# A planned order of TensorE work: later due times for FFN transposes and first scores, and a last update in two pieces

## Chip, cores and metric

The kernel runs on one core of a Trainium2 chip. The metric is the device time of one execution in microseconds. All weights (some 220 MB) stream from HBM once per execution.

## The reference

Two blocks on x of 256 tokens by 1024, in float32. The first has two layers, each:

```
x = x + 0.5 * swiglu(rms_norm(x, ffn1_norm), w_gate, w_up, w_down)
h = rms_norm(x, mix_norm)
pa, pb, pc, pd = split(h @ w_in)
ya, yb, yc, yd = neighbourhood(pa), latent(pb), differential(pc), grouped(pd)
x = x + concat(ya, yb, yc, yd) @ w_out
x = x + 0.5 * swiglu(rms_norm(x, ffn2_norm), ...)
x = rms_norm(x, final_norm)
```

swiglu is (silu(h @ w_gate) * (h @ w_up)) @ w_down with an inner width of 2816. The four mixers are attentions of four heads each over all 256 tokens, with different norms, biases and rotations. The second block is one layer of three gated branches (pooling, windowed attention with sinks, causal attention), `x + merged @ w_out`, and a last rms_norm, which gives the output.

## The kernel before, in words

**Products.** Every large product is made in three matmuls of fp32r: weights and activations are split into a high part and a rest (hi, lo and xTh, xTl), and hi·hi, hi·lo and lo·hi are added up in PSUM (`acc`, L339). A matmul takes 128 rows of the inner dimension, one token tile t (128 tokens; there are two) and up to 512 output columns. Weights come in units of 128 x 1024 (512 KB): a transfer on SyncE's queue into one of three staging buffers `st`, then a "cut": ScalarE writes hi, VectorE writes lo (`Weights.cut`, L194). Six pairs hi/lo are alive at a time.

**The stages of a layer.** `ffn` (L546) goes over six chunks of 512 (the last 256) inner columns; for each it makes the gate product and the up product for both token tiles with `proj` (L496). `ev_gate` (L553) writes fg = silu(gate) on ScalarE; `ev_up` (L557) writes fh = up * rstd * fg on VectorE into one buffer per token tile, and spawns the transposes of fh: `trans_split` (L394) transposes four 128 x 128 tiles on TensorE into a PSUM tile tps, from which ScalarE writes hTh and VectorE hTl. When all chunks are done, `wide` (L521) makes the down product from hTh and hTl over 22 rows of tiles. `mixers` (L712) makes the input projections of the four head groups in the order differential, latent, neighbourhood, grouped, and spawns a generator for each; the output projection is again `wide` over eight row tiles in the order 4, 5 (differential), 2, 3 (latent), 0, 1 (neighbourhood), 6, 7 (grouped), each as soon as its rows yT are there (`before`, L1072). The next FFN starts with the gate product of token tile 0.

**A head group.** `softmax_pv` (L572) works through jobs (a pair of heads and a token tile): `scores` (two PSUM tiles sps, row maximum on VectorE, exponential E on ScalarE), `transposes` of E (evicted as PT), `values` (evicted as yt), `finish` (transposed back into y). When a token tile's jobs are done, `post` normalises y to yn and transposes it into yT. A group takes the turn at L673 (`att["busy"]`) and gives it back when the transposes of its last job are issued (L701). The second block has two such groups, `moba` (L1178) and `swa` (L1199).

**The order of the work.** The program is written out in one order by a planner. `Clock` (L61) estimates, for TensorE, ScalarE, VectorE and GpSimd, when each operation would end; `clock.pe` is its TensorE time and `clock.last` the estimated end of what an eviction or a step issued. A generator given to `spawn` (L410) has a due time: at the first opportunity after `clock.pe` has passed it, its next step is issued between the matmuls of the running product (`tick`, L446, called after each three or six matmuls). By default the due time is `clock.last`. Transfers count as arriving 1.4 us apart. `drain_until` (L453) runs background steps until a condition holds and moves the planner's TensorE time ahead if nothing is due. The framework then orders each engine's queue by program order and by what its own estimate has ready; operations that read PSUM are lifted by 14 places (L151 to L153).

**The end.** `last` (L1308) takes each finished piece of the last product (t, h), h the half of 512 columns: VectorE adds it to x, ScalarE squares it with a running sum, VectorE multiplies by the final gain into xg. After h = 1 the two sums are added, scaled and raised to -0.5 on GpSimd (`rpow`, L348), VectorE scales the first half and SyncE sends it, ScalarE scales the second and sends it from its own queue. In a row of the trace, L153 and L154 are the helper through which all VectorE, ScalarE and GpSimd operations go (with and without a PSUM operand), L333 is every matmul and L337 every transpose.

Of the kernel before, what the change touches and what calls it, by code (L numbers as in the profile page):

```python
# [10 lines left out]
F = mybir.dt.float32  # L11
R = mybir.dt.float32r
ACTF = mybir.ActivationFunctionType
ALU = mybir.AluOpType
# [3 lines left out]
D = 1024  # L18
DFF = 2816
L = 2  # L20
EPS = 1e-6
# [18 lines left out]
FIRST = [1, 1, 2, 2, 2]  # L40
WARM = 6
AHEAD = 14
OUT_ORDER = (4, 5, 2, 3, 0, 1, 6, 7)
IN2 = {"ax": 0, "az": 512, "bq": 1024, "bkv": 1536, "bz": 1792,
       "cq": 2304, "ck": 2816, "cv": 3328, "cz": 3840, "g": 4352}
# [79 lines left out]
class Engine:  # L125
# [5 lines left out]
    def __getattr__(self, op):  # L131
        f = getattr(self._eng, op)

        def call(*args, **kw):
# [16 lines left out]
            if not sb:  # L151
                with self._tc.high_priority(AHEAD):
                    return f(*args, **kw)  # L153
# [76 lines left out]
def decoder(ctx, tc, a, out):  # L230
    nc = tc.nc
    clock = Clock()
    act, dve, gps = (Engine(e, n, clock, tc) for e, n in (
        (nc.scalar, "act"), (nc.vector, "dve"), (nc.gpsimd, "pool")))
    PSUM = bass.MemoryType.PSUM

    def pool(name, bufs, stack=ctx, **kw):
        return stack.enter_context(tc.tile_pool(name=name, bufs=bufs, **kw))
# [13 lines left out]
    stat = pool("stat", 3)  # L252
# [6 lines left out]
    mhalf = const.tile([128, 16], F, name="mhalf")  # L259
# [4 lines left out]
    for l in range(L):  # L264
        for f in (1, 2):
            if f == 2:
# [8 lines left out]
                ws.add(wi, 8, 512, 2, (OFF_GQA, OFF_GQA + 512))  # L275
                for k in OUT_ORDER:
                    ws.add(a["w_out"][l][k * 128:(k + 1) * 128, :], 1, D, 1)
            for c in range(0, DFF, 512):
                n = min(512, DFF - c)
# [13 lines left out]
    x = keep.tile([128, 2, D], F, name="x")  # L293
# [11 lines left out]
    def tok(t):  # L305
        return slice(t * 128, (t + 1) * 128)

    def half(h):
        return slice(h * 512, (h + 1) * 512)
# [16 lines left out]
    def load_gain(ap):  # L326
        g = gain_p.tile([128, D], F, tag="g", name="gain")
        nc.sync.dma_start(out=g, in_=ap.partition_broadcast(128))
        return g
# [18 lines left out]
    def rpow(ss, n, inv, tag):  # L348

        m = stat.tile([128, n], F, tag=f"m{tag}{n}", name="ms")  # L350
        dve.tensor_scalar(m, ss, inv, EPS, op0=ALU.mult, op1=ALU.add)
        r = stat.tile([128, n], F, tag=f"r{tag}{n}", name="r")
        if n < 4:
            gps.tensor_tensor(out=r, in0=m, in1=mhalf[:, :n], op=ALU.pow)
            return r
        I = mybir.dt.int32
        dve.tensor_scalar(r.bitcast(I), m.bitcast(I), -0.5, float(0x5f3759df), op0=ALU.mult,
                          op1=ALU.add)
        q = stat.tile([128, 16], F, tag="q", name="q", bufs=1)[:, :n]
        for _ in range(3):  # L360
            dve.scalar_tensor_tensor(out=q, in0=m, scalar=-0.5, in1=r, op0=ALU.mult,
                                     op1=ALU.mult)
            dve.tensor_tensor(out=q, in0=q, in1=r, op=ALU.mult)
            dve.scalar_tensor_tensor(out=r, in0=q, scalar=1.5, in1=r, op0=ALU.add, op1=ALU.mult)
        return r

    def square_sum(src, tag):
        junk = junk_p.tile([128, D], mybir.dt.bfloat16, tag="junk", name="junk")
        ss = stat.tile([128, 1], F, tag="ss" + tag, name="ss")
        act.activation(out=junk[:, :src.shape[1]], in_=src, func=ACTF.Square, accum_out=ss)  # L370
        return ss
# [7 lines left out]
    def scaled(out, ps, s):  # L379
        act.activation(out=out, in_=ps, func=ACTF.Copy, scale=s)  # L380
# [29 lines left out]
    def spawn(gen, first=False, at=None):  # L410
        at = clock.last if at is None else at
        bg.insert(0 if first else len(bg), [gen, at, at])

    def timed(f, *args):

        before, clock.last = clock.last, 0.0
        f(*args)
        end = clock.last
        clock.last = max(before, end)
        return end  # L420
# [21 lines left out]
    def step(f, *args):  # L442
        f(*args)
        yield
# [101 lines left out]
    def ffn(norm_out, first=None):  # L546
        hTh = big.tile([128, KF, S], R, tag="bigA", name="hTh")
        hTl = big.tile([128, KF, S], R, tag="bigB", name="hTl")
        for c in range(6):
            n = min(512, DFF - 512 * c)  # L550
            g = {}

            def ev_gate(t, ps):  # L553
                g[t] = wk.tile([128, 512], F, tag=f"fg{t}", name="fg", bufs=1)
                act.activation(out=g[t][:, :n], in_=ps[:, :n], func=ACTF.Silu, scale=rstd[t])

            def ev_up(t, ps):  # L557
                h = wk.tile([128, 512], F, tag=f"fh{t}", name="fh", bufs=1)
                dve.scalar_tensor_tensor(out=h[:, :n], in0=ps[:, :n], scalar=rstd[t],
                                         in1=g[t][:, :n], op0=ALU.mult, op1=ALU.mult)  # L560
                ks = slice(4 * c, 4 * c + n // 128)
                spawn(step(trans_split, hTh[:, ks, tok(t)], hTl[:, ks, tok(t)], h[:, :n]), True)

            proj(8, n, first if first and c == 0 else 1024 // n, ev_gate, skew=c == 0)
            proj(8, n, 1024 // n, ev_up)
        wide(range(KF), hTh, hTl, [1] * (KF - 4) + [4],
             lambda t, h, ps: norm_out.update(t, h, ps, 0.5), lambda k, t: k < KF - 2 or not bg)
# [4 lines left out]
    def softmax_pv(jobs, post, scored=None, have_v=lambda: True):  # L572
# [3 lines left out]
        n = len(jobs)  # L576
# [95 lines left out]
        e_at, p_at, y_at = {}, {}, {}  # L672
        yield lambda: not att["busy"]  # L673
        att["busy"] = True
        while i4 < n:
            now = clock.pe
            nxt = [now + 300]
            if i4 < i3:
                nxt.append(y_at[i4])
            if i3 < i2:  # L680
                nxt.append(p_at[i3])
            if i2 < i1:
                nxt.append(e_at[i2])
            if i4 < i3 and y_at[i4] <= now:
                end = timed(finish, i4)
                t = jobs[i4]["t"]
                if post and (i4 == n - 1 or jobs[i4 + 1]["t"] != t):
                    spawn(post(t), True, end)
                i4 += 1
                yield 0  # L690
            elif i3 < i2 and p_at[i3] <= now and i3 == i4 and have_v():
                y_at[i3] = timed(values, i3)
                att["pt"] -= 1
                i3 += 1
                yield 0
            elif i2 < i1 and att["pt"] < 2 and e_at[i2] <= now:
                p_at[i2] = timed(transposes, i2)
                att["pt"] += 1
                i2 += 1
                if i2 == n:  # L700
                    att["busy"] = False  # L701
                yield 0
            elif i1 < n and i1 - i2 < 2 and (i1 == 0 or e_at[i1 - 1] <= now + 300):
                e_at[i1] = timed(scores, i1)
                i1 += 1
                if i1 == n and scored:
                    scored()
                yield 0
            else:
                yield max(now + 100, min(nxt))  # L710

    def mixers(l, cols, rows, nlam, norm_out):  # L712
# [108 lines left out]
        def latent(um, w):  # L821
# [96 lines left out]
            for t in range(2):  # L918
                for p in range(2):
# [4 lines left out]
                        v=[[v[:, k, h, 0:64] for k in range(2)] for h in hs],  # L924
                        y=heads(y[:, t, tok(p)])))
            yield from softmax_pv(jobs, post_rms(y, "mla_beta", 2), lambda: finished.add("mla_s"))

        def differential(u, v):
# [143 lines left out]
        def before(k, t):  # L1072
            k0 = k // 2 * 2
            return (k0, t) in finished and (k0 == 6 or (k0, 1) in finished)
        wide(OUT_ORDER, yTh, yTl, [1] * 4 + [4], lambda t, h, ps: norm_out.update(t, h, ps, 1.0),
             before)
# [20 lines left out]
    for l in range(L):  # L1097
        ffn(Norm(gains[:, 3 * l + 1]), FIRST if l == 0 else None)
        if l == 0:
            nc.sync.dma_start(out=cst, in_=a["cst"].rearrange("(t p) c -> p t c", p=128))  # L1100
            for n in (3, 6):
                dve.tensor_tensor(out=gains[:, n], in0=gains[:, n], in1=gains[:, 7 + n // 6],
                                  op=ALU.mult)
# [200 lines left out]
            fin2.add("c")  # L1304
    gf = load_gain(a["final_norm_g_2"])
    ss, xg = {}, {}

    def last(t, h, ps):  # L1308
        sl = x[:, t, half(h)]
        dve.tensor_tensor(out=sl, in0=ps, in1=sl, op=ALU.add)  # L1310
        ss[t, h] = square_sum(sl, f"x{h}")
        if h == 0:
            xg[t] = xg_p.tile([128, D], F, tag="xg", name="xg")
        dve.tensor_tensor(out=xg[t][:, half(h)], in0=sl, in1=gf[:, half(h)], op=ALU.mult)
        if h == 1:
            dve.tensor_tensor(out=ss[t, 0], in0=ss[t, 0], in1=ss[t, 1], op=ALU.add)
            r = rpow(ss[t, 0], 1, 1.0 / D, f"x{t}")
            dve.tensor_scalar(xg[t][:, half(0)], xg[t][:, half(0)], r, None, op0=ALU.mult)
            nc.sync.dma_start(out=out[tok(t), half(0)], in_=xg[t][:, half(0)])
            scaled(xg[t][:, half(1)], xg[t][:, half(1)], r)  # L1320
            nc.scalar.dma_start(out=out[tok(t), half(1)], in_=xg[t][:, half(1)])

    wide(range(8), mTh, mTl, [4, 4], last)


# [118 lines left out]
```

## Time and profile before

| what | value |
|---|---|
| median of 3 runs | 1319.79 us (1315.48 to 1320.84) |
| the profiled execution, its own time | 1318.63 us |
| its span, first to last instruction | 1316.5 us |
| TensorE busy | 1291.3 us, 98% |
| weight loads (beside the matmuls) | 1046.1 us, 79% |
| VectorE, ScalarE, GpSimd busy | 792.7, 722.5, 28.6 us |
[...]
| transfers | 221.80 MB, 168 GB/s |

The profiled execution spent 1318.63 - 1316.5 = 2.1 us outside its span. Busy time of a matmul overlaps with the next, so groups of matmuls are read by the time from start to start: 0.227 us for 512 columns at the full clock. A row of a timeline gives the start, the duration, the engine, and in brackets the idle time of the engine before it and what ended it.

### The profile page before, as it was taken

The page shows a single profiled execution, that of the slowest core. Times are in us where ns is not written, and L with a number is a line of the kernel's source. Part 1 is how long each engine was busy: PE and PEld are TensorE (multiplying, and loading weights), DVE is VectorE, ACT ScalarE, POOL GpSimd, SP SyncE. Part 2 cuts the span into 40 slices and gives each one's busy share as a digit, 9 for nine tenths or more (in the row PEclk, how much of TensorE's full clock was granted, in tenths as well). Part 3 has the DMA queues.
Part 4 walks back from the last instruction along what each step waited for, and adds up shares of the span by engine and source line. Part 5 has one row for each costly group of instructions (what it writes and reads, how often), then busy time and mean ns, then how long its engine had stood idle before and what let it go on. Part 6 is the DMA issues. An engine that isn't in the chain of part 4 may idle for free.

```text
span 1316.5 us, 17826 instructions
## 1 busy us (share of the span) xinstructions
PE 1291.3 (98%) x6514; PEld 1046.1 (79%) x6514; DVE 792.7 (60%) x1615; ACT 722.5 (55%) x1223; POOL 28.6 (2%) x44
## 2 busy tenths in 40 slices
PE   8999999999999999999999999999999999999997
PEld 7788888766788888788888876678888887678886
DVE  5655449895655544755545798565554565555475
ACT  6544437866644444644435676664444466566543
POOL 0000001000000000100000000000000000000000
PEclk9999999999999999999999998999999999999999
DMA  8766657432566665666665733156667474245652
GB/s 278 219 181 188 183 166 238 126 97 65 172 190 184 183 188 164 208 183 188 186 186 167 218 115 98 45 179 189 185 181 235 144 234 127 80 145 168 205 170 80
DMA packets 109815, 221.80 MB, mean 168 GB/s; under 512 B 7456, under 2 KB 30368, under 8 KB 109728
## 3 DMA queue, kind: packets, MB, share of 16 engines
q1 hardware_dynamic: 109152, 220.04, 55.5%
q8 instruction: 51, 0.84, 0.3%
q10 hardware_dynamic: 576, 0.63, 0.1%
q14 instruction: 36, 0.29, 0.1%
HBM read 219.59 MB, written 1.05 MB: 168 GB/s over the span
## 4 chain that ended last, share of the span: by engine, by line
PE 82%; DMA 6%; DVE 5%; ACT 4%; issue 1%; POOL 1%; SPq 0%; POOLq 0%; ACTq 0%; DVEq 0%
PE mmps L333 71%; PE tps L337 6%; PE sps L333 3%; DMA st<-in_w_in_dram 3%; PE tps L333 3%; DVE lo L154 2%; ACT hi L154 2%; DMA st<-in_ffn_w_gate_dram 2%; DMA st<-in_ffn_w_up_dram 1%; DVE xTl L153 1%; ACT junk L154 1%; ACT xTh L153 1%; POOL r L154 1%; DVE x L153 0%; DVE qkT L153 0%
## 5 line engine op out<-in xcount | busy, mean ns | idle before, releaser
L154 DVE TENSOR_TENSOR lo<-st,hi 128x1024 fp32r<-128x1024 f32 (+2 forms) x403 | 488.2, 1214 | 395.3 <-ACT hi L154 394.5
L154 ACT ACTIVATE hi<-st 128x1024 fp32r<-128x1024 f32 (+2 forms) x403 | 421.9, 1050 | 427.6 <-PE mmps L333 348.8
L333 PE MATMUL mmps<-hi,xTh 128*128 128x512 f32 (+2 forms) x1200 | 451.9, 377 | 1.0 <-ACT xTh L153 1.0
L333 PE MATMUL mmps<-hi,xTl 128*128 128x512 f32 (+2 forms) x1200 | 446.3, 372 | 0.0
L333 PE MATMUL mmps<-lo,xTh 128*128 128x512 f32 (+2 forms) x1200 | 446.2, 372 | 0.0
L333 PEld LDWEIGHTS mmps<-hi,xTh 128*128 128x128 f32 x1200 | 226.1, 188 | 42.4 <-issue 2.5
L333 PEld LDWEIGHTS mmps<-hi,xTl 128*128 128x128 f32 x1200 | 226.2, 188 | 38.2 <-issue 0.5
L333 PEld LDWEIGHTS mmps<-lo,xTh 128*128 128x128 f32 x1200 | 226.3, 189 | 36.2 <-issue 1.0
L333 PE MATMUL mmps<-lo,hTh 128*128 128x512 f32 x352 | 138.1, 392 | 0.0
L333 PE MATMUL mmps<-hi,hTh 128*128 128x512 f32 x352 | 137.8, 392 | 0.0
L333 PE MATMUL mmps<-hi,hTl 128*128 128x512 f32 x352 | 113.6, 389 | 0.0
L333 PE MATMUL mmps<-hi,yT 128*128 128x512 f32 (+1 forms) x248 | 89.0, 416 | 0.6 <-ACT yT L153 0.6
L333 PEld LDWEIGHTS mmps<-hi,hTl 128*128 128x128 f32 x352 | 66.1, 188 | 13.6
L333 PEld LDWEIGHTS mmps<-hi,hTh 128*128 128x128 f32 x352 | 66.1, 188 | 13.6
L333 PEld LDWEIGHTS mmps<-lo,hTh 128*128 128x128 f32 x352 | 66.1, 188 | 13.1
L154 POOL TENSOR_TENSOR r<-ms,mhalf 128x1 f32<-128x1 f32 x40 | 28.4, 711 | 1283.1 <-DVE ms L154 1283.0
L333 PEld LDWEIGHTS mmps<-hi,yT 128*128 128x128 f32 x248 | 46.1, 190 | 11.4 <-ACT yT L153 1.9
L333 PE MATMUL mmps<-lo,yT 128*128 128x512 f32 (+1 forms) x124 | 49.7, 401 | 0.0
L154 ACT ACTIVATE E<-E,nm 128x256 f32<-128x256 f32 (+1 forms) x80 | 38.3, 480 | 14.9 <-DVE nm L154 14.7
L153 ACT ACTIVATE fg<-mmps,r 128x512 f32<-128x512 f32 (+1 forms) x48 | 31.1, 652 | 21.7 <-PE mmps L333 21.7
L153 ACT ACTIVATE xTh<-tps,gains 128x128 fp32r<-128x128 f32 x112 | 31.6, 365 | 15.5 <-PE tps L337 15.5
L153 ACT ACTIVATE PT<-tps 128x512 f32<-128x512 f32 (+1 forms) x56 | 27.9, 502 | 21.4 <-PE tps L337 20.8
(172 smaller groups left out, 1035.0 us busy)
## 6 DMA issues: line engine op xcount, KB each, us to landing
st<-in_w_in_dram SPq DMA_DIRECT2D x90, 512.0 KB, 4.0
st<-in_ffn_w_up_dram SPq DMA_DIRECT2D x88, 512.0 KB, 4.0
st<-in_ffn_w_down_dram SPq DMA_DIRECT2D x88, 512.0 KB, 3.6
st<-in_ffn_w_gate_dram SPq DMA_DIRECT2D x87, 512.0 KB, 3.8
st<-in_w_out_dram SPq DMA_DIRECT2D x24, 512.0 KB, 3.7
st<-in_w_in_dram SPq DMA_DIRECT2D x8, 416.0 KB, 4.2
scratch<-in_t5b_dram SPq DMA_DIRECT2D x4, 512.0 KB, 5.1
scratch<-in_nab_dram SPq DMA_DIRECT2D x4, 512.0 KB, 7.3
```

The lines of the kernel that those rows point to most:

```text
L153: return f(*args, **kw)
L154: return f(*args, **kw)
L333: nc.tensor.matmul(ps, lhsT=lhsT, rhs=rhs, start=start, stop=stop)
L337: nc.tensor.transpose(ps, src, ident)
```

## The change

A constant MARGIN of 1500 (ns of the planner's time) is added. The transposes of fh get the due time `clock.last + MARGIN` in place of `clock.last`. Each head group, having taken its turn, yields `clock.pe + MARGIN` once before its first scores. `last` hands pieces to a new function `piece`: the four (t, h) as before, but (1, 1) as two pieces of 256 columns. The gain multiply takes in the factor sqrt(1024), so that the sum of squares needs only a constant added; the last addition of sums and that constant are one operation. VectorE scales 640 columns and ScalarE 384 (before 512 and 512), and SyncE and ScalarE send as many.

```diff
+MARGIN = 1500.0
...
-                spawn(step(trans_split, hTh[:, ks, tok(t)], hTl[:, ks, tok(t)], h[:, :n]), True)
+                spawn(step(trans_split, hTh[:, ks, tok(t)], hTl[:, ks, tok(t)], h[:, :n]), True,
+                      clock.last + MARGIN)
...
         att["busy"] = True
+        yield clock.pe + MARGIN
         while i4 < n:
...
+    cut = 640
 
     def last(t, h, ps):
-        sl = x[:, t, half(h)]
-        dve.tensor_tensor(out=sl, in0=ps, in1=sl, op=ALU.add)
-        ss[t, h] = square_sum(sl, f"x{h}")
+        for c in (0, 256) if (t, h) == (1, 1) else (0,):
+            piece(t, h, ps[:, c:c + 256] if (t, h) == (1, 1) else ps, c)
+
+    def piece(t, h, ps, c):
+
+        n = ps.shape[1]
+        sl = slice(512 * h + c, 512 * h + c + n)
+        dve.tensor_tensor(out=x[:, t, sl], in0=ps, in1=x[:, t, sl], op=ALU.add)
+        s = square_sum(x[:, t, sl], "y" if c else f"x{h}")
         if h == 0:
             xg[t] = xg_p.tile([128, D], F, tag="xg", name="xg")
-        dve.tensor_tensor(out=xg[t][:, half(h)], in0=sl, in1=gf[:, half(h)], op=ALU.mult)
-        if h == 1:
-            dve.tensor_tensor(out=ss[t, 0], in0=ss[t, 0], in1=ss[t, 1], op=ALU.add)
-            r = rpow(ss[t, 0], 1, 1.0 / D, f"x{t}")
-            dve.tensor_scalar(xg[t][:, half(0)], xg[t][:, half(0)], r, None, op0=ALU.mult)
-            nc.sync.dma_start(out=out[tok(t), half(0)], in_=xg[t][:, half(0)])
-            scaled(xg[t][:, half(1)], xg[t][:, half(1)], r)
-            nc.scalar.dma_start(out=out[tok(t), half(1)], in_=xg[t][:, half(1)])
+        dve.scalar_tensor_tensor(out=xg[t][:, sl], in0=x[:, t, sl], scalar=float(D) ** 0.5,
+                                 in1=gf[:, sl], op0=ALU.mult, op1=ALU.mult)
+        if sl.stop < D:
+            if t in ss:
+                dve.tensor_tensor(out=s, in0=s, in1=ss[t], op=ALU.add)
+            ss[t] = s
+            return
+        m = stat.tile([128, 1], F, tag=f"mx{t}1", name="ms")
+        dve.tensor_scalar(m, s, ss[t], D * EPS, op0=ALU.add, op1=ALU.add)
+        r = stat.tile([128, 1], F, tag=f"rx{t}1", name="r")
+        gps.tensor_tensor(out=r, in0=m, in1=mhalf[:, :1], op=ALU.pow)
+        dve.tensor_scalar(xg[t][:, :cut], xg[t][:, :cut], r, None, op0=ALU.mult)
+        nc.sync.dma_start(out=out[tok(t), :cut], in_=xg[t][:, :cut])
+        scaled(xg[t][:, cut:], xg[t][:, cut:], r)
+        nc.scalar.dma_start(out=out[tok(t), cut:], in_=xg[t][:, cut:])
```

## Rows read from the trace of the kernel before

**Rows 1.** The page: the span, and each engine's busy time

```profile
span 1316.5 us, 17826 instructions
PE 1291.3 (98%) x6514; PEld 1046.1 (79%) x6514; DVE 792.7 (60%) x1615; ACT 722.5 (55%) x1223; POOL 28.6 (2%) x44
```

**Rows 2.** Windows: length, busy of PE, PEld, DVE, ACT, POOL; clock, DMA, GB/s

```profile
279.00:338.00 59.00, 55.31 (x335) 38.35 (x334) 41.55 (x166) 38.37 (x114) 3.50 (x7) 0.97 0.22 68
...
350.00:550.00 200.00, 199.45 (x950) 166.06 (x950) 110.50 (x126) 96.82 (x119) 4.03 (x4) 1.00 0.63 187
```

**Rows 3.** Waits: us in total, times, longest us

```profile
PEld tps L337 <- DVE fh L153: 6.3, 11, 2.2
...
PE sps L333 <- ACT E L153: 4.6, 8, 1.1
...
PE tps L337 <- DVE fh L153: 2.9, 2, 1.8
...
PE sps L333 <- ACT qkT L153: 2.3, 2, 1.9
```

**Rows 4.** Timeline of TensorE, first FFN, second chunk

```profile
54.92 0.39 PE L333 MATMUL mmps<-hi,xTl 128*128 128x512 f32 x1
57.08 1.31 PE L337 MATMUL tps<-ident,fh 128*128 128x128 f32 x8 [1.77 <-DVE fh L153]
```

**Rows 5.** Timeline of VectorE, the same place

```profile
56.28 1.40 DVE L153 SCALAR_TENSOR_TENSOR fh<-mmps,r,fg 128x512 f32<-128x512 f32 x2
```

**Rows 6.** Timeline of ScalarE, the same place

```profile
54.04 1.06 ACT L154 ACTIVATE hi<-st 128x1024 fp32r<-128x1024 f32 x1 [0.99 <-DMA st<-in_ffn_w_up_dram]
```

**Rows 7.** Timeline of TensorE, third FFN, first chunk

```profile
552.43 0.40 PE L333 MATMUL mmps<-lo,xTh 128*128 128x512 f32 x1
553.94 0.66 PE L337 MATMUL tps<-ident,fh 128*128 128x128 f32 x4 [1.11 <-DVE fh L153]
```

**Rows 8.** Timeline of TensorE, first scores of the first and second layer

```profile
227.19 0.38 PE L333 MATMUL sps<-qkT 32*128 32x256 f32 x2 [0.45 <-ACT qkT L153]
...
744.97 0.28 PE L333 MATMUL mmps<-hi,xTl 128*128 128x256 f32 x1
747.12 0.39 PE L333 MATMUL sps<-qkT 32*128 32x256 f32 x2 [1.86 <-ACT qkT L153]
```

**Rows 9.** Timeline of TensorE, first layer, scores of the second head group

```profile
284.70 1.50 PE L333 MATMUL sps<-kT,qT 96*128 96x256 f32 x4 [1.14 <-ACT E L153]
...
287.76 0.99 PE L333 MATMUL mmps<-hi,yT 128*128 128x512 f32 x1
```

**Rows 10.** Timeline of TensorE, end of the first layer's output projection

```profile
335.33 0.50 PE L333 MATMUL mmps<-hi,xTh 128*128 128x512 f32 x1 [0.50 <-ACT xTh L153]
...
336.37 0.50 PE L333 MATMUL mmps<-hi,yT 128*128 128x512 f32 x1 [0.32 <-ACT yT L153]
```

**Rows 11.** Windows, TensorE alone: length, busy, granted clock, DMA share, GB/s

```profile
286.00:288.00 2.00, 2.00 (x10) 0.50 0.00 0
...
805.00:808.00 3.00, 3.00 (x11) 0.50 0.00 0
```

**Rows 12.** Timeline of all engines after the last matmul

```profile
1309.31 0.69 DVE L153 TENSOR_TENSOR x<-mmps,x 128x512 f32<-128x512 f32 x1 [1.00 <-PE mmps L333]
...
1310.09 0.63 ACT L154 ACTIVATE junk<-x 128x512 bf16<-128x512 f32 x1 [1.73 <-DVE x L153]
1310.63 0.19 ACT L154 ACTIVATION_READ_ACCUMULATOR junk<-x 128x1 f32 x1
1310.85 0.16 DVE L154 TENSOR_TENSOR ss<-ss 128x1 f32<-128x1 f32 x1
1311.04 0.15 DVE L154 TENSOR_SCALAR ms<-ss 128x1 f32<-128x1 f32 x1
1311.34 0.55 POOL L154 TENSOR_TENSOR r<-ms,mhalf 128x1 f32<-128x1 f32 x1 [4.89 <-DVE ms L154]
1311.92 0.72 ACT L154 ACTIVATE xg<-xg,r 128x512 f32<-128x512 f32 x1 [1.10 <-POOL r L154]
1311.92 0.49 DVE L154 TENSOR_SCALAR xg<-xg,r 128x512 f32<-128x512 f32 x1 [0.73 <-POOL r L154]
```

**Rows 13.** Groups by line and shape: busy us, mean ns of 256 columns

```profile
L153 DVE TENSOR_TENSOR qkT<-tps,qkT 128x256 fp32r<-128x256 f32 x8 | 3.3, 418 | 0.0
L154 ACT ACTIVATE junk<-um 128x256 bf16<-128x256 f32 x4 | 1.7, 415 | 0.1
```

## The prediction

> **What bounds the kernel now.** I read the page first: in a span of 1316.5 us TensorE is busy for 98% [rows 1], so only its idle time, about 25 us, is there to win. The stages of the windows say where that lies: the 200 us of an FFN stretch hold 199.45 us of TensorE work, the 59 us in which the first layer's attention ends hold 55.31 [rows 2]. So an FFN stretch is set by TensorE, and any stall removed there shortens the end; the end of the mixers is set by a chain through all engines, and a stall removed there may only move. The list of waits then names the two stalls that this change aims at: weight loads (and matmuls behind them) waiting for fh, which VectorE writes, and the first scores waiting for qkT [rows 3]. Together with scores waiting for E they are the largest entries of TensorE.
>
> How such a stall comes about is in the timelines. TensorE's queue is a fixed order. [...] VectorE wrote fh only at 56.28 to 57.68 [rows 5], behind a weight cut whose ScalarE half had waited 0.99 us for its transfer [rows 6]. The planner counts with transfers that arrive on time, so its due time was early.
>
> **The change part by part.**
>
> *Transposes of fh due 1.5 us later.* No instruction is added. 44 tiles in each of four FFNs give 176 transposes, in 48 groups; each moves behind some seven matmuls (1.5/0.227), to the next place where background work is looked at. No DMA and no SyncE or GpSimd work moves with them directly; ScalarE's and VectorE's two evictions per group come later by the same time, and the next reader of hTh and hTl is the down projection, tens of us later. fh has one buffer per token tile, rewritten one chunk later (16 us or more), so nobody waits for that. What can be won: at least the 2.9 us in which TensorE was idle, at most the 6.3 us of the weight loads [rows 3]; nothing, if VectorE is late by the margin too. From start to start the two long waits cost 1.93 us [rows 4] and 1.28 us (1.51 from the matmul at 552.43 to the transposes, less the pace) [rows 7]; the nine short ones I put at 0.6 together, since a matmul runs on under most of a 0.3 us weight-load wait. In rows 4 the delay was longer than the margin, but the background is looked at only every third matmul (0.68 us), which adds something to the margin. **-3.8 us**, bounds -6.3 and 0.
>
> *First scores due 1.5 us later, ten groups.* In the layers' first group the scores waited for qkT: 1.86 us idle at 747.12 (2.0 from start to start) and 0.45 at 227.19 (0.6) [rows 8]. Seven matmuls now go first, so TensorE does that work earlier. But the scores start no sooner: qkT lands when it lands, in layer 1 they now start up to 0.9 us later than it. And what TensorE has done ahead it lacks later: at 284.70 it waits 1.14 us for E, and the next matmul of the output projection comes only at 287.76, when the first group's last result is normalised and transposed [rows 9]. The stretch before it has no filler. So a gain there is largely handed back. Bounds -2.6 (all kept) and +1.5 (the first group's end comes later by the margin, nothing kept); I take **0**.
>
> *The other groups of a layer.* They run one after the other, for one may start its scores only when the one before has issued its last transposes. Each now sits for 1.5 us while it holds the turn. For the second group there is no filler, so in the queue its scores come next all the same; the third and fourth lose 1.5 us each, 3.0 us a layer, at the end of the chain. What covers it: next to the wait for the last yT the queue already holds gate matmuls of the next FFN (335.33, ahead of yT at 336.37) [rows 10]. Two of the twelve that two weight units and one token tile allow ran there; ten more are 2.3 us. Left: 0.7 us in each of two layers, **+1.4 us**. Upper bound +6 (no cover). Lower bound -7.1: the eight waits of scores for E (4.6 us) [rows 3] go, because the second group no longer meets the evictions of the third group's qkT, and with them the stretches at a granted clock of 0.50, which cost half of 2 and of 3 us [rows 11]. In the second block's two groups there is filler throughout (projections follow for 100 us), and their delay costs nothing; if that cover were gone, 1.5 us each.
>
> *The tail.* Now: add 0.69 from 1309.31, square whose sum is read at 1310.63 for 0.19, two small sums of 0.16 and 0.15, power, then the scaling of 512 columns in 0.72 and the transfer [rows 12]. After: two adds of 256 columns, 0.42 each [rows 13], overlapping by 0.09 as fh's pair does [rows 5], so the second ends near 0.75; reads of PSUM are lifted in the queue (L152), so it goes ahead of the gain multiply. The first square starts at 0.5 and the second (0.42 [rows 13] less its overlap with the read) near 1.05, its sum is there at about 1.55 against 1.51 now. One small sum falls away (-0.19), but the second multiply now stands ahead of the last one on VectorE and ends about then. ScalarE scales 384 columns for 512 (-0.1), VectorE 640 in some 0.57, still under ScalarE. Sum -0.25 to +0.5 (the second add behind the first multiply and the small sum); **-0.1 us**. [...]
>
> **Sum.** -3.8 + 0 + 1.4 - 0.1 = -2.5 us. The profiled execution took 1318.6 us with launch, so 1316.1; the median of the three runs, 1319.8, lies 1.2 us above it and gives 1317.3. I state 1316.7.
>
> **Rivals.** What a measurement can tell from no change is about 0.5%, 6.6 us.
>
> *Faster by more: the head groups fall clear of each other.* The 1.5 us take the scores of the second group past the eight evictions of the third group's qkT on ScalarE and VectorE, so E comes in time and the clock stays up. For: the waits for E are the largest of TensorE [rows 3], and the clock falls right after them, and only there inside the kernel [rows 11]. [...] Against: without filler the queue has nothing to put in between. All of it gives -3.8 - 2.6 - 7.1 = -13.5, 1305; about half, which I think likelier, 1310. Chance 0.25.
>
> *Slower: the turn between the groups.* Place: TensorE's wait for the last yT [rows 10]. If the three groups after the first are each late by 1.5 us and the gate matmuls don't cover it (their accumulators are those of the output projection), each layer ends 4.5 us later, and a second stretch at half clock after that wait, as long as that of rows 11, adds 1 to 1.5: +11.5 - 3.8 = +7.7, 1327. It decides once the wait for yT grows beyond 5 us a layer. Against: only 0.32 us of waiting is there now. Chance 0.10.
>
> *It does next to nothing.* The queues are not the program's order: rows 10 show matmuls of the next FFN ahead of earlier ones. If the ordering takes the transposes whenever its own estimate has fh ready, a later due time changes few places and the waits stay: 1319.5. Chance 0.17.
>
> *The forecast*: 0.48.
>
> Faster 0.25 is the second case; same is the forecast and the inert case, 0.65; slower 0.10. The range leaves out the lower part of the faster rival and the slower one: 1308 to 1324. For the forecast alone it is 1313 to 1321 (fh -6.3 and no give-back; fh kept at half and +3 at the mixers' ends).
>
> **What would show it.** Right: waits for fh on TensorE and its weight loads nearly gone, and the FFN stretches shorter by 1 to 2 us each in the first and third FFN; the idle 1.86 us before the second layer's first scores down to about 0.5; the stretch from there to the next FFN no shorter; the last chain from VectorE's add to the last transfer the same within 0.5 us. Wrong: waits for fh still over 3 us, or the mixers' ends shorter or longer by more than 3 us a layer, or a clock below 1.00 in other places than rows 11.

## The result, and the profile after

The changed kernel takes 1334.9 us (median of six runs, 1333.9 to 1342.1) against 1320.3 for the kernel before on the same chip: ratio 1.0128, 95% interval 1.0107 to 1.0149. By the ratio it is slower by some 17 us (14 to 20); the medians lie 14.6 us apart, the two profiled spans 15.2. The forecast was 1316.7 within 1308 to 1324, so sign and range were both missed. In the changed kernel line numbers are one higher: the helper is L155 (L154 where it lifts a read of PSUM), matmuls L334, transposes L338.

The page of the profiled execution (1333.9 us), to be held against [rows 1]:

```profile
span 1331.7 us, 17837 instructions
PE 1300.9 (98%) x6514; PEld 1054.7 (79%) x6514; DVE 797.9 (60%) x1616; ACT 727.1 (55%) x1227; POOL 26.9 (2%) x44
```

TensorE's share is still 98%. It does the same 6514 instructions and is "busy" 9.6 us longer, so part of the loss is in slower instructions. The list of waits, TensorE and its weight loads, against [rows 3]:

```profile
PE sps L334 <- ACT E L154: 10.0, 4, 4.1
PE tps L338 <- DMA x<-in_x_dram: 2.2, 3, 1.2
PE tps L338 <- DVE q L155: 1.9, 2, 0.9
...
PEld tps L338 <- DVE fh L154: 0.4, 1, 0.4
```

The waits for fh (2.9 and 6.3 us before) and for qkT (2.3) are gone, as meant. The wait of scores for E has grown from 4.6 us in eight pieces to 10.0 in four. Windows (columns as in [rows 2]) of an FFN stretch, of the end of the first layer's mixers, and of one place inside it:

```profile
350.00:550.00 200.00, 199.60 (x959) 167.09 (x958) 114.09 (x140) 104.28 (x135) 4.59 (x5) 1.00 0.61 187
280.00:348.00 68.00, 61.56 (x349) 42.26 (x348) 39.94 (x157) 39.19 (x118) 3.85 (x7) 0.92 0.12 35
289.00:302.00 13.00, 11.41 (x45) 8.16 (x46) 6.39 (x30) 6.21 (x18) 0.00 (x0) 0.61 0.00 1
```

The end of the mixers, 59 us with 55.3 of TensorE work before [rows 2], has become 68 with 61.6, at a mean granted clock of 0.92. To find the stages' lengths I take the starts of the last matmul on hTh (end of an FFN's down projection) and the last on yT (end of a layer's output projection). In the first layer these are, before and after:

```profile
198.88 0.39 PE L333 MATMUL mmps<-hi,hTh 128*128 128x512 f32 x1
...
339.93 0.40 PE L333 MATMUL mmps<-hi,yT 128*128 128x512 f32 x1
```

```profile
197.10 0.39 PE L334 MATMUL mmps<-hi,hTh 128*128 128x512 f32 x1
...
350.19 0.39 PE L334 MATMUL mmps<-hi,yT 128*128 128x512 f32 x1
```

So the first mixer stage went from 141.0 to 153.1 us. The same for all stages, from the traces:

| stage, us | before | after | difference |
|---|---|---|---|
| first FFN (from the start) | 198.9 | 197.1 | -1.8 |
| mixers, layer 1 | 141.0 | 153.1 | +12.0 |
| FFNs two, three, four | 187.1, 190.4, 187.1 | 185.4, 188.8, 185.4 | -1.7, -1.6, -1.6 |
| mixers, layer 2 | 143.9 | 152.8 | +8.9 |
| second block, to the last mTh matmul | 260.0 | 261.4 | +1.3 |
| tail | 8.07 | 7.67 | -0.4 |

The FFNs gave 6.6, the mixers of the two layers took 20.9. Inside the first mixer stage two places are late. First, the differential group, which takes the turn first: its scores begin at 226.94 (227.19 before [rows 8]) but end at 270.95, where they ended at 261.28. TensorE hardly waited in between (1.0 us, 0.5 before). What changed is the order in its own queue. A layer has 288 projection matmuls (those that read xTh or xTl), a third of which read xTl. Windows with the xTl matmuls alone (columns as in [rows 11]), from behind the group's first scores to its last, and from there to the latent group's first, before:

```profile
227.50:261.50 34.00, 11.30 (x33) 1.00 0.45 133
261.50:279.70 18.20, 6.06 (x15) 1.00 0.56 170
```

and after:

```profile
227.50:271.20 43.70, 16.16 (x45) 1.00 0.49 150
271.20:280.00 8.80, 0.00 (x0) 0.81 0.39 120
```

With all three products, 144 of the 288 stood ahead of the group's first scores, 99 between first and last, and 45 behind, which kept TensorE at work while the group ended. Now it is 153, 135 and 0, in both layers. The price is paid behind this group. Counted from the last hTh matmul, the latent group's first scores are late by only 2.1 us (1.1 in layer 2). From there to the last yT matmul it takes 70.1 us where it took 60.1 (69.4 for 61.6).

Second, the latent group behind it, whose scores wait for E:

```profile
280.09 0.60 PE L334 MATMUL sps<-kT,qT 96*128 96x256 f32 x2
...
284.55 0.70 PE L334 MATMUL sps<-kT,qT 96*128 96x256 f32 x2
...
289.95 2.07 PE L334 MATMUL sps<-kT,qT 96*128 96x256 f32 x4 [4.07 <-ACT E L154]
```

ScalarE's exponential there waited 2.82 us for the row maximum nm, which VectorE wrote only behind the preparation of the grouped-query heads (ug, pr):

```profile
288.06 0.56 DVE L155 TENSOR_TENSOR ug<-ug,r 128x384 f32<-128x384 f32 x1
288.53 0.16 DVE L155 SCALAR_TENSOR_TENSOR r<-q,r 128x4 f32<-128x4 f32 x1
288.60 0.29 DVE L155 TENSOR_TENSOR pr<-ug,prt 128x128 f32<-128x128 f32 x1
288.80 0.16 DVE L155 SCALAR_TENSOR_TENSOR q<-ms,r 128x4 f32<-128x4 f32 x1
288.87 0.43 DVE L154 TENSOR_REDUCE nm<-sps 128x1 f32<-128x256 f32 x1
...
289.33 0.47 ACT L154 ACTIVATE E<-sps,nm 128x256 f32<-128x256 f32 x1 [2.82 <-DVE nm L154]
```

This is the group's third row maximum, 8.8 us after its first scores. Before, it came 3.25 us after them:

```profile
279.79 0.38 PE L333 MATMUL sps<-kT,qT 96*128 96x256 f32 x1
...
283.04 0.42 DVE L153 TENSOR_REDUCE nm<-sps 128x1 f32<-128x256 f32 x1
```

VectorE was not slower (0.43 us for a row maximum, 0.42 before) and hardly idle (busy for 8.59 of the 9.30 us from 280.00 to 289.30). It had other things first.

The theory from this (A): the hold after taking the turn makes nothing wait on the chip, since it adds no instruction. It lets other work go ahead of the group: preparation and weight cuts in VectorE's and ScalarE's queues, and projections in TensorE's. Its rivals: B, the later FFN transposes reorder the mixers; the turn between the groups, that is, three later groups late by 1.5 us each; D, scores that are late by 1.5 us ten times; the half clock; and E, a bad draw that any shift can bring.

### The profile page after: what moved, and what is told of

It is laid out like the page before. It is cut to its first block, busy times and chain, and to the rows that moved or that the text cites. A ratio compares the mean times of both kernels' runs of the same rounds, so it can differ in the third digit from the quotient of the medians.

```text
span 1331.7 us, 17837 instructions
## 1 busy us (share of the span) xinstructions
PE 1300.9 (98%) x6514; PEld 1054.7 (79%) x6514; DVE 797.9 (60%) x1616; ACT 727.1 (55%) x1227; POOL 26.9 (2%) x44
## 4 chain that ended last, share of the span: by engine, by line
PE 89%; DVE 5%; DMA 3%; ACT 2%; issue 1%; POOL 1%; POOLq 0%; ACTq 0%; DVEq 0%
PE mmps L334 77%; PE tps L338 6%; PE sps L334 3%; PE tps L334 3%; DMA st<-in_w_in_dram 1%; DVE lo L155 1%; POOL r L155 1%; DVE xTl L154 1%; ACT hi L155 1%; DMA x<-in_x_dram 0%; DMA st<-in_ffn_w_gate_dram 0%; DVE x L154 0%; DVE yn L155 0%; DMA st<-in_ffn_w_up_dram 0%; ACT xTh L154 0%
## 5 line engine op out<-in xcount | busy, mean ns | idle before, releaser
L155 DVE TENSOR_TENSOR lo<-st,hi 128x1024 fp32r<-128x1024 f32 (+2 forms) x403 | 488.0, 1214 | 378.2 <-ACT hi L155 376.6
L155 ACT ACTIVATE hi<-st 128x1024 fp32r<-128x1024 f32 (+2 forms) x403 | 422.6, 1052 | 398.6 <-PE mmps L334 318.1
L334 PE MATMUL mmps<-hi,xTh 128*128 128x512 f32 (+2 forms) x1200 | 451.8, 377 | 0.0
L334 PE MATMUL mmps<-hi,xTl 128*128 128x512 f32 (+2 forms) x1200 | 446.3, 372 | 0.0
L334 PE MATMUL mmps<-lo,xTh 128*128 128x512 f32 (+2 forms) x1200 | 445.6, 372 | 0.0
L334 PEld LDWEIGHTS mmps<-hi,xTh 128*128 128x128 f32 x1200 | 226.6, 189 | 40.7 <-issue 2.5
L334 PEld LDWEIGHTS mmps<-hi,xTl 128*128 128x128 f32 x1200 | 226.4, 189 | 38.5 <-issue 1.0
L334 PEld LDWEIGHTS mmps<-lo,xTh 128*128 128x128 f32 x1200 | 226.8, 189 | 35.9 <-issue 0.3
L334 PE MATMUL mmps<-lo,hTh 128*128 128x512 f32 x352 | 137.9, 392 | 0.0
L334 PE MATMUL mmps<-hi,hTh 128*128 128x512 f32 x352 | 137.6, 391 | 0.0
L334 PE MATMUL mmps<-hi,hTl 128*128 128x512 f32 x352 | 113.7, 390 | 0.0
L334 PE MATMUL mmps<-hi,yT 128*128 128x512 f32 (+1 forms) x248 | 89.4, 418 | 0.1
L334 PEld LDWEIGHTS mmps<-hi,hTh 128*128 128x128 f32 x352 | 66.1, 188 | 13.6
L334 PEld LDWEIGHTS mmps<-hi,hTl 128*128 128x128 f32 x352 | 66.1, 188 | 13.6
L334 PEld LDWEIGHTS mmps<-lo,hTh 128*128 128x128 f32 x352 | 66.1, 188 | 13.2
L334 PEld LDWEIGHTS mmps<-hi,yT 128*128 128x128 f32 x248 | 47.7, 196 | 11.4 <-issue 2.1
L155 POOL TENSOR_TENSOR r<-ms,mhalf 128x1 f32<-128x1 f32 x40 | 26.7, 669 | 1300.2 <-DVE ms L155 1300.2
L334 PE MATMUL mmps<-lo,yT 128*128 128x512 f32 (+1 forms) x124 | 51.7, 417 | 0.0
L334 PE MATMUL sps<-kT,qT 64*128 64x256 f32 (+2 forms) x144 | 37.2, 393 | 10.0 <-ACT E L154 10.0
L155 ACT ACTIVATE E<-E,nm 128x256 f32<-128x256 f32 (+1 forms) x80 | 38.4, 481 | 9.4 <-DVE nm L155 9.3
L154 ACT ACTIVATE PT<-tps 128x512 f32<-128x512 f32 (+1 forms) x56 | 28.0, 503 | 27.9 <-PE tps L338 27.7
L154 ACT ACTIVATE xTh<-tps,gains 128x128 fp32r<-128x128 f32 x112 | 31.5, 367 | 20.7 <-PE tps L338 20.7
```

Source lines behind the costliest of these rows:

```text
L334: nc.tensor.matmul(ps, lhsT=lhsT, rhs=rhs, start=start, stop=stop)
```

## The experiments

Ratios are to the kernel before on the same chip, with the 95% interval. Diffs are against the kernel before with `MARGIN = 1500.0` added, unless said.

### The parts apart

The FFN part alone:

```
+ ... hTl[:, ks, tok(t)], h[:, :n]), True, clock.last + MARGIN)
```

> Only the later due time of the FFN's transposes; no wait after taking the turn, tail as before. Theory A (the wait in the first head group, the differential one, sets the mixers back): the four FFN stretches keep their gain of 1.8, 1.3, 1.6 and 1.3 us and the mixers are as before, so 1320.3 - 6.0 = about 1314; first mixer from its first wide matmul to the next FFN about 141 us, as before. Theory B (the shift of the FFN's transposes alone reorders the mixers behind them): about 1333, the first two mixers 153 us each.

Measured 0.9938 (0.9916 to 0.9961), 8 us faster. Its FFN stretches are shorter by 0.6, 1.1, 1.9 and 1.2, and its mixers are no longer (140.0 and 140.7 us). B falls.

The hold alone, in all ten groups:

```
         att["busy"] = True
+        yield clock.pe + MARGIN
```

> Only the wait of 1.5 us that each head group makes after it has taken the turn, FFNs and tail as before. Theory A: mixers 12.0 and 8.9 us longer as in the changed kernel, second block +1.3, FFNs unchanged: 1320.3 + 22 = about 1341. Theory B: within 2 us of the kernel before, 1319 to 1322. Theory C (it needs both, each alone is harmless): likewise near 1320.

Measured 1.0162 (1.0130 to 1.0193), 21 us slower, with mixers of 151.6 and 153.0. The hold is the whole loss: 21 less 6 to 8 for the FFNs is the 13 to 15 that, within the interval, the whole change lost. The hold in the differential group only:

```
+        if diff:
+            yield clock.pe + MARGIN
```

> The wait only in the differential group of each layer, the first to take the turn; FFNs and tail as before. Theory A: nearly the whole loss, 1320.3 + 17 to + 21, so 1337 to 1341, and the eight differential jobs take about 44 us from first to last score where they took 34. Rival (the turn between the groups: the three later groups lose 1.5 us each and the clock falls): no loss here, 1319 to 1322, the jobs in 34 us.

and in all others only:

```
+        if not diff:
+            yield clock.pe + MARGIN
```

> The wait only in the groups after the first of each layer and in the second block's two; FFNs and tail as before. Theory A: little, 1320.3 + 1 to + 4 (second block +1.3 in the changed kernel, the third and fourth group of a layer some tenths to 1.5 us each). Rival (the turn between the groups): the whole loss here, 1336 to 1341.

Measured 1.0130 (1.0095 to 1.0164) and 1.0117 (1.0080 to 1.0153). The first is as A said, with 44 us from the differential group's first score to its last, and with the projections in the order 153, 135, 0. With the hold in the others their order is 144, 99, 45, as before the change. The rival (the turn between the groups) had no loss in the first kernel, so it is not the whole cause. The second result is not as A said: I had it at +1 to +4 and it is +15, a microsecond below the range that the rival gave it. So both costs are real, and they don't add up: 17 + 15 apart, 21 together. In the trace with the hold in the later groups everything up to the latent group's first scores stands as before, 1.78 us later throughout (281.57 for 279.79, because the first FFN, which is the same in both, ended later by as much); those scores issue in the same place. Then:

```profile
284.12 0.42 DVE L154 TENSOR_REDUCE nm<-sps 128x1 f32<-128x256 f32 x1
...
285.19 0.48 PE L334 MATMUL sps<-kT,qT 96*128 96x256 f32 x1 [2.35 <-ACT E L154]
```

against, in the kernel before:

```profile
280.44 0.42 DVE L153 TENSOR_REDUCE nm<-sps 128x1 f32<-128x256 f32 x1
...
281.51 0.48 PE L333 MATMUL sps<-kT,qT 96*128 96x256 f32 x1 [0.46 <-ACT E L153]
```

The row maximum starts 2.55 us after its scores where it took 0.65. This is A at a second place: here TensorE's queue is unchanged, VectorE's is not. I had looked for A only in the first group.

### What gets ahead

Here every group holds for 1.5 us, but nothing else is planned meanwhile except projections:

```
+        hold["e"] = hold["cur"]
+        yield clock.pe + MARGIN
+        hold["e"] = None
...
-            if is_ready(e):
+            if is_ready(e) and hold["e"] in (None, e):
...
-        if ws.can_cut():
+        if ws.can_cut() and hold["e"] is None:
...
+                e = hold["e"] or min(...)
```

> The wait of 1.5 us in all ten groups, FFNs and tail as before, but while a group waits no other background step and no weight cut is put into the queues; projections alone go on. Theory A (on the chip nothing sits still; what costs is the work of VectorE and ScalarE that the wait lets into their queues ahead of the group's first softmax): the loss falls from 20 us to under 6, 1319 to 1327. Rival D (the scores are simply 1.5 us late, ten times, with nothing to cover them): still 1335 to 1342. The half clock between the groups, 12 us worth in the kernel with the wait alone against 4.8 before, goes with the loss under A.

Measured 1.0033 (1.0012 to 1.0054), 4 us. The same hold, without what it let in, costs a fifth. D falls. The projections stand in the order 153, 90, 45. In the trace the mixers take 143.3 and 144.0 us and the half clock came down (6.8 us worth), but this execution, 1319.0 us, is the fastest of ten with a median of 1324.0. The next two ask which work it was. Background steps may go, weight cuts not:

```
-        if ws.can_cut():
+        if ws.can_cut() and not hold["on"]:
```

> The wait of 1.5 us in all groups; weight cuts are kept out while a group waits, other background steps (preparation and evictions of other groups) may go. A1 (the weight cuts of 1.05 and 1.22 us are what gets ahead): near the kernel in which nothing else goes, 1320 to 1328. A2 (the preparation and evictions of the other groups are): near the wait alone, 1335 to 1343.

and cuts may go, background steps not (the diff with hold["e"], without its change to can_cut):

> The converse: while a group waits weight cuts may go, other background steps may not. A1: 1335 to 1343. A2: 1320 to 1328. If it takes both, both kernels lie near 1324.

Measured 1.0052 (1.0031 to 1.0072) and 1.0130 (1.0105 to 1.0154). A1 holds for most of it: with the cuts kept out 7 us are left of 21, with the cuts alone let in it is 17. The order of the projections goes with it: 153, 90, 45 with the cuts kept out, 153, 135, 0 with the cuts alone let in. How a cut does that in the plan is argued and not shown. By the kernel, scores are issued only when the planner expects the exponentials of the job before, and a cut takes time on both engines that make those. How many cuts run between the differential group's first and last scores in the first layer shows in the groups by line of that stretch (busy us, mean ns | idle). With cuts alone let in (230.8 to 274.2):

```profile
L155 DVE TENSOR_TENSOR lo<-st,hi 128x1024 fp32r<-128x1024 f32 x12 | 14.7, 1222 | 1.8 <-ACT hi L155 1.5 <-issue 0.3
L155 ACT ACTIVATE hi<-st 128x1024 fp32r<-128x1024 f32 x12 | 12.7, 1056 | 6.5 <-PE mmps L334 5.0 <-DMA st<-in_w_in_dram 1.3
```

With cuts alone kept out (229.7 to 262.4):

```profile
L155 DVE TENSOR_TENSOR lo<-st,hi 128x1024 fp32r<-128x1024 f32 x7 | 8.6, 1223 | 1.6 <-ACT hi L155 1.6
L155 ACT ACTIVATE hi<-st 128x1024 fp32r<-128x1024 f32 x9 | 9.4, 1052 | 1.7 <-DMA st<-in_w_in_dram 1.6
```

Before, VectorE had eight there (9.8 us, one under way at the start) and ScalarE nine (9.5 us); in the changed kernel twelve and twelve (14.7 and 12.7 us). With 7 or 8 cuts the group took 32.5 to 34 us, with 12 it took 43 to 44. That count alone proves little, as a longer stretch holds more cuts; the two kernels do. What is left without cuts (+7) fits the second group's place: its first row maximum starts 2.58 us after its scores there, as with the hold in the later groups, and 0.63 where cuts alone are let in. One more run has the hold in the second group alone:

```
+        att["n"] += 1
+        if att["n"] in (2, 6):
+            yield clock.pe + MARGIN
```

> The wait only in the second (latent) group of each layer. Theory A (queues): in the kernel with the waits of all later groups, its scores kept their place on TensorE (281.57, 1.78 after before, as everything ahead of it) while its first row maximum started 2.55 us after them where it was 0.65; that alone gives 1.9 us a layer and a longer half clock, 1322 to 1329. If the third and fourth group carry the loss of that kernel: 1318 to 1322.

Measured 1.0054 (1.0029 to 1.0080), +7, and the same 2.55 us from the first scores to their maximum. So the first group's cost comes of the weight cuts that the hold lets in, and the second's of other heads' preparation. Of the 15 us of all later groups, 7 are this one's; how the rest divides between the third, the fourth and the second block (+1.4 in its trace) was not tried apart.

A longer hold, `MARGIN = 3000.0`:

> Only the wait, 3.0 us in place of 1.5, FFNs and tail as before. Theory A (more of the others' work gets ahead): slower than with 1.5 us, 1342 to 1355. Rival E (any shift of the plan is a draw, and 1.5 us drew badly): anything from 1316 to 1345, below 1336 as likely as above.

Measured 1.0153 (1.0110 to 1.0196): as with 1.5, not worse. It speaks against a lucky or unlucky draw, though one value cannot rule it out, and A's growth with the margin did not come either. The first layer's differential group had twelve cuts there as well, and the projections the order 159, 129, 0: with 1.5 us the order had already tipped, and more delay added nothing.

### Is it the half clock?

Taking busy time times the missing share of the clock, window by window of 1 us, the half clock (a granted clock of 0.50) covers 4.8 us of TensorE's work before, 13.9 after and none with the FFN part alone. That would be 9 of the 17 us. So the next kernel has the hold and, wherever the plan has TensorE waiting, matmuls of the identity into an unused part of a scores' bank, to keep it busy:

```
+                for _ in range(int((e[1] - clock.pe) // 220) if 0 in spare else 0):
+                    mm(spare[0], ident, ident, True, True)
                 clock.wait_pe(e[1])
```

> The wait of 1.5 us in all groups, weight cuts and all else allowed, and wherever the plan has TensorE waiting for a background step it gets matmuls of the identity into an unused part of a scores' bank, 0.22 us each by the plan. Clock theory (of the 20 us about 12 are half clock, which follows the gaps): TensorE is busy through them, the clock stays up, 1328 to 1334. Chain theory (the gaps are set by VectorE and ScalarE, the clock adds little): 1337 to 1345, the extra matmuls at most in the way.

Measured 1.0195 (1.0174 to 1.0216). The windows of the place between the groups in both layers, with the hold alone:

```profile
284.00:304.00 20.00, 15.26 (x68) 10.52 (x67) 13.39 (x70) 9.91 (x29) 0.00 (x0) 0.74 0.00 1
810.00:834.00 24.00, 19.26 (x89) 13.52 (x88) 16.93 (x84) 11.84 (x34) 0.00 (x0) 0.78 0.02 8
```

and filled, with the largest filling on TensorE's timeline:

```profile
284.00:304.00 20.00, 18.88 (x139) 16.19 (x138) 13.23 (x67) 8.99 (x27) 0.00 (x0) 1.00 0.00 1
810.00:834.00 24.00, 22.85 (x154) 19.39 (x154) 17.28 (x86) 10.55 (x33) 0.00 (x0) 0.94 0.06 20
```

```profile
291.95 4.96 PE L335 MATMUL sps<-ident 128*128 128x128 f32 x42 [1.12 <-ACT E L154]
```

The clock stays at its upper level nearly throughout there (1.00 and 0.94, where it was 0.74 and 0.78), and the mixers take 153.1 and 153.7 us, where they took 151.6 and 153.0. So filling the gaps does not win the time back. It does not show that the half clock is free, since the filling stands in the same queue as the chain: the latent group's fifth row maximum starts 15.24 us after its first scores, where with the hold alone it was 11.42. What part of the 17 us is the clock stays open.

### The better kernel

The FFN part and the tail, without the hold:

> The changed kernel without the wait after the turn: FFN transposes later and the tail in two pieces. Theory A (the waits of the head groups carry the whole loss, the other two parts only gain): as the kernel with the FFN part alone (0.9938 of before) less 0.4 for the tail (8.07 to 7.67 us from the last mTh matmul to the end of the span), so 0.990 to 0.995 of the kernel before, about 1311. If the parts only work together: over 1318.

Measured 0.9942 (0.9923 to 0.9961), 1311.2 us: faster than before and about 24 us below the changed kernel. It is the version to keep; the edits below are made to it. FFN transposes 3.0 us later in place of 1.5, otherwise the same:

> FFN transposes due 3.0 us later, where the change has 1.5, tail in two pieces, no wait after the turn. If 1.5 us already took all waits for fh (none of over 0.6 us left with the FFN part alone), the same within 2 us as with 1.5: 1309 to 1313. If some of the gain is luck in where the groups fall: more than 4 us apart from it.

Measured 0.9950 (0.9928 to 0.9973), no different. Then three attempts to better it. With a quiet hold in the differential group alone:

```
+        if diff:
+            hold["e"] = hold["cur"]
+            yield clock.pe + MARGIN
+            hold["e"] = None
```

> FFN transposes later and the tail in two pieces, and a wait of 1.5 us in the differential group alone, in which nothing else goes into the queues. With nothing else issued, that group took 32.5 us from its first to its last score where it took 34.1 before. If that reaches the end of the mixers: up to 1.6 us a layer faster than without the wait, 1308 to 1310. If it is handed back at the next wait, as forecast for the first group's scores: 1310 to 1313, no different.

Measured 0.9981 (0.9966 to 0.9997): 5 us given away, though the group itself took 34.1 and 33.5 us; both expectations missed. The mixers were 147.1 and 144.5. The trace shows one place: the latent group's first row maximum starts 1.94 us after its scores, as with the quiet hold in all groups (1.95), where it is 0.65 without a hold. Why was not followed further. With the filling:

> FFN transposes later and the tail in two pieces, no wait after the turn, the same filling. Clock theory: the 3.4 us that the half clock costs in the kernel without filling go, 1306 to 1309. If the filling stands ahead of work that is ready: 1311 to 1318.

Measured 0.9991 (0.9977 to 1.0005): the second of its cases: the clock was up throughout (a mean of 0.999, no half clock but in the tail), and the mixers took 142.9 and 143.0 us against 140.8 and 142.0. The filling costs more than the clock gives. It delays the chain here too: the latent group's third row maximum comes 5.59 us after its first scores, 3.26 without the filling. With fewer cuts during a turn:

```
-        if ws.can_cut():
+        if ws.can_cut() and not (att["busy"] and len(ws.ready) > 1):
```

> FFN transposes later and the tail in two pieces, no wait after the turn; while a head group has the turn no weight is cut as long as two cut units are ready. If cuts between a group's jobs cost by themselves: 1304 to 1309. If they only cost where the wait lets them in: 1310 to 1314. If weights come late: over 1316.

Measured 1.0018 (1.0002 to 1.0035), by its time the third of its cases: mixers of 148.3 and 149.0 us, and the differential group in 37.7. But weight loads wait only 0.2 us for a cut weight in this trace. What grew are waits for what VectorE prepares (4.7 us for yn). So keeping the cuts out longer is no gain, and why is not shown.

## Why the prediction was wrong

**FFN transposes: right, undersized.** I put -3.8 with -6.3 as the far end. The last three FFNs gave 1.6 each in the changed kernel and 1.1 to 1.9 alone; with the first FFN, whose start also waits for x (2.5 us of TensorE's idle time before, 2.2 in the changed kernel), 4.8 to 6.6 in all. The two long waits were priced from start to start and went. The nine short ones, put at 0.6 "together, since a matmul runs on under most of a 0.3 us weight-load wait", were worth two to three microseconds: the four FFNs gained nearly alike, while long waits stood in two. By the ratio the part alone gave 8. Where the other 2 or 3 lie is open. One place may be the first FFN, which a single trace does not fix: it takes 197.3 to 201.2 us in the ten traces with the FFNs as before (median 200.2), 196.1 to 198.3 in the seven with later transposes (197.2).

**First scores of the first group: the step that failed.** "Bounds -2.6 and +1.5; I take 0." Measured alone +17. I had the kind of loss, "what TensorE has done ahead it lacks later", and its size from the margin: seven matmuls, and a group's end later by 1.5 us at most. Nine more did go ahead of the first scores. But the 45 that had stood behind the group's last scores went ahead of them too, 10 us of work at 0.227 each in place of 1.5. The last scores came 9.7 us later, and nothing was left to cover what follows. What I did not follow is the plan of VectorE and ScalarE, by which the later scores get their place: with weight cuts (1.22 us of VectorE and 1.06 of ScalarE each) kept out of the hold, the 45 stay behind. I had a row for it: a weight cut ahead of the late fh is what [rows 5, 6] show. I had used it for the FFN and not here.

**The other groups: wrong in kind.** "Each now sits for 1.5 us while it holds the turn." Nothing sits on the chip. "For the second group there is no filler, so in the queue its scores come next all the same" is true of TensorE, where they did stand in the same place, and beside the point: on VectorE they did not. The forecast cost was 1.4, the upper bound 6, the measured one 15 alone. The upper bound was drawn from a time of waiting; it had to be drawn from the work at hand for the other engines. For the second group that is other heads' preparation (first row maximum 1.9 us later, +7 alone); for the rest it stays open.

**The tail: right, small.** Forecast -0.1, measured -0.4, past my far end of -0.25. The rows that answer to [rows 12]:

```profile
1324.91 0.76 DVE L154 TENSOR_TENSOR x<-mmps,x 128x256 f32<-128x256 f32 x2 [1.14 <-PE mmps L334]
...
1326.30 0.19 ACT L155 ACTIVATION_READ_ACCUMULATOR junk<-x 128x1 f32 x1
1326.52 0.21 DVE L155 TENSOR_SCALAR ms<-ss 128x1 f32<-128x1 f32 x1
1326.81 0.55 POOL L155 TENSOR_TENSOR r<-ms,mhalf 128x1 f32<-128x1 f32 x1 [4.95 <-DVE ms L155]
1327.39 0.62 ACT L155 ACTIVATE xg<-xg,r 128x384 f32<-128x384 f32 x1 [0.91 <-POOL r L155]
1327.40 0.55 DVE L155 TENSOR_SCALAR xg<-xg,r 128x640 f32<-128x640 f32 x1 [0.66 <-POOL r L155]
```

From the last add to the scaling it is 2.48 us (2.61 before), the scaling 0.62 (0.72), and from its start to the end of the span 4.31 (4.58); what of that is not the scaling, 0.17 us, lies behind the last issue, and why is not shown: from issue to landing ScalarE's transfers took 2.6 us for 192 KB and 2.5 for 256 KB before (medians of two). The two adds take 0.76 us together where one took 0.69, and the last sum is read 1.39 us after the add's start (1.32 before). So the split cost the chain 0.07 us, and the small sum that fell away more than paid for it (0.51 us from that read to GpSimd's start, 0.71 before).

**The rivals.** The faster one saw the right place, scores waiting for E between the groups, and the wrong direction: 1.5 us did not take the scores clear of the third group's evictions, it put other groups' preparation ahead of their row maxima. The slower one had the right sign, the half clock and three uncovered groups, at a chance of 0.10. But its place, the wait for the last yT, stayed out of the largest waits, and its price, 1327, was 8 us short, because it too was made of lateness on TensorE. Of the signs named for a wrong forecast, "the mixers' ends shorter or longer by more than 3 us a layer" is what happened.

**The sum with the measured parts:** FFNs -6, hold +21, tail -0.4, that is +15; measured +17 (14 to 20).

## What to carry to other kernels

A later due time in a planned schedule is no wait. It is a change of order, and on every queue that the step feeds. Price it by what the planner has at hand for the other engines in that time, here weight cuts of more than a microsecond on each of two engines and another group's preparation, and not by the time itself. Then count on the bottleneck's own queue how much filler stands ahead of, among and behind the steps of the chain (144, 99, 45 against 153, 135, 0 here). Give slack to a step that others wait for little (the FFN transposes: in the first FFN of the kernel before they start at 35.2 to 139.3 us, and the first matmul that reads hTh at 137.8), and none to the head of a chain.

## What was not expected of the hardware

The half clock seems to cost about what it covers where nothing is put in its place. Four kernels have the mixers in the same order: before, the FFN part alone, and the better kernel with 1.5 and with 3.0 us. In the second layer their traces have 3.1, 0, 1.7 and 3.4 us of TensorE's work at half clock, and the mixers take 143.9, 140.7, 142.0 and 143.5 us. Executions of one kernel say the same: in the 26 of the kernel before that ran beside the better kernel, time and mean granted clock go together, from 1316.0 us at 0.998 to 1325.0 at 0.989. A fitted line gives about 1.1 us for each 0.001 of the clock, near to 0.001 of the span, 1.3 us. Both can also follow from one late input, so this is no proof that the clock is the cause. Between the groups the half clock came with waits: in the changed kernel the granted clock was 0.79 from 289 to 290, where the wait of 4.07 us ended, and 0.50 from 290 to 299; in the kernel before it was 0.69 from 285 to 286, behind the wait of 1.14 us [rows 9], and 0.50 from 286 to 288. Not every wait brought it: in the kernel before it stayed 1.00 through the 1.77 us idle for fh [rows 4] and the 1.86 us for qkT [rows 8]. What brings it is not shown.

Raising the clock by filling is another matter. With the hold it went from a mean of 0.986 to 0.995 over the span, and the time stayed or grew, because the filling delayed the chain. One kernel's runs can also lie further apart than the effects in question: the hold in the second group alone ran from 1318.6 to 1332.7 us, and its trace is of the slowest.
